# Order of the small matrix products in a one-core RWKV-7 and band-attention step: 64-row and 32-row products issued in turn on different parts of the TensorE array

## The chip, the cores and the metric

The kernel runs on one core of one Trainium2 chip. The metric is the device time of one execution in microseconds (us); lower is better. Engines are named as the profile names them: PE is TensorE's products, PEld its weight loads, DVE is VectorE, ACT is ScalarE, POOL is GpSimd, SP is the engine whose queue issues nearly all DMAs. Times inside an execution are microseconds from the start of its span.

## What is computed

One inference step of a two-layer encoder for two request groups: a prompt of 1024 tokens, and 8 sequences of 16 new tokens that continue older states. The width is 1024, with 16 heads of 64 features in both layers.

```python
# layer 0: recurrence with a 64x64 state a head
sa = einsum('bhij,bhj->bhi', s, a_t)
s  = s * w_t[:, :, None, :] + sa[..., None] * b_t[:, :, None, :] + v_t[..., None] * k_t[:, :, None, :]
y  = einsum('bhij,bhj->bhi', s, r_t)
out = (group_norm(y) + bonus) * g @ w_o
# layer 1: attention over the own chunk of 64 tokens and the 8 chunks before it
s = einsum('bqhd,bkhd->bhqk', q_b, k_b) * scale + bias
p = softmax(where(allowed, s, NEG_INF))
o = einsum('bhqk,bkhd->bqhd', p, v_b)
# after each mix
x = x + gt_f * (silu(h @ w_gate) * (h @ w_up)) @ w_down
```

All arithmetic is fp32; the large products split each operand into a high part and a rest in a one-pass format (`F32R`), and the small ones are plain fp32 products, which the trace shows as two weight loads and two products each.

## The kernel before, in words

**Stages.** From 0 to about 1420 us: layer 0's projections in three blocks of 384 tokens (the third holds the last 256 of the prompt and the 128 of the samples), with the recurrence of earlier blocks beside them. Then the output projection, the gated feed-forward (1545 to 2400 us), keys, values and first queries (to 2640 us), the attention (2640 to 3210 us), and the second feed-forward.

**The recurrence** works on windows of 128 tokens, two chunks `c` of 64 tokens each, and on half of the heads at a time: four feature tiles `f`, each with two heads `e` (rows 0 to 63 and rows 64 to 127). There are 9 windows `w` (the last holds the samples) and so 18 units. `inverses` prepares a triangular inverse a chunk. `win_prep` (line 714) loads a unit's operands and makes the pairwise products `G` (lines 738 to 747: products with 64 rows and 128 columns of the array, four of one head half into a bank, then two DVE copies under a mask out of it), then transposes `BK` (lines 750 to 757). The banks of tag `G` are two. `win_state` (line 838) carries the state over a chunk with products `X`, `U`, `D` in banks of tag `st`, which take the two heads of a feature tile in turn on the left and the right half of the array's columns. `win_y` (line 902) sums a unit's output in one bank `Y`: for each `c`, `f`, `e` first a product over 128 rows (`YL`, `UV`) and at once the product of the state over 64 rows (`XL`, `S`; for the samples four products of 16 columns with `ssv`) onto the same columns. `win_post` normalises `Y`. `windows` weaves a unit's run with the end of the unit before, and prepares two units ahead.

**The attention** goes through eight pairs of heads (`pair`, line 1548). A tile is 128 queries `qt` of one head `e` against up to five blocks of keys. `advance` (line 1580) is a pipeline of tiles: at each step the new tile's scores (banks `S`) and exponentials, the output products of the tile three steps older, two steps of a later pair's queries (banks `acc`), then the transposes into `PT` (one buffer) and their copy to `pts` (two buffers, line 1633) of the tile one step older. The tile's output (line 1637) is up to five products in a row into the 64 columns of its own head. The order of a pair's 16 tiles is written out at line 1564: the second head one block of queries behind the first. After the first head's last tile the next pair's second head of keys and queries is loaded and split (`kprep`, `qprep`, lines 1426 and 1437). Two groups of four sample sequences a pair (`sample_group`, line 1667) enter the same pipeline; their output takes, for each sequence `b`, four products over 128 rows (`vc`, `pts`) into that sequence's quarter of 32 columns and one over 16 rows (`vn`, `pts`) onto it. The cache tiles `kc` and `vc` have one buffer each.

**What sets the order.** The kernel is written in a tile language that makes all waits and buffer assignments. Its planner replays the program in a simulated time before it is compiled, and lets each engine's queue take what is ready, the earlier in the code first. So the order in the code is a priority, and the order on an engine can differ from it. Each engine then runs its own queue in order.

Of the kernel before, what the change touches and what calls it, by code (L numbers as in the profile page):

```python
# [21 lines left out]
# ---------------------------------------------------------------- constants  # L22
# [54 lines left out]
def prep(i):  # L77
    i = {k: np.asarray(v) for k, v in i.items()}
    d = {}
# [7 lines left out]
    # groups of 16 tokens, each behind the token before it  # L87
# [17 lines left out]
    st = i["state_wkv"][0].transpose(3, 1, 0, 2)  # j, h, b, i  # L105
# [35 lines left out]
class Trunk:  # L141
# [11 lines left out]
    # ------------------------------------------------------------ set-up  # L153
# [34 lines left out]
    # ------------------------------------------------------------ adaLN  # L188
    def step(self, n=1):
        """n loads of the adaLN products that run beside other work"""  # L190
        for _ in range(n):
            next(self.ada, None)

    def ada_steps(self, units, tag="aux", bufs=1):
        """modulations, 512 features a unit: [128, 4, prompt and 8 sequences]; a quarter of a bank's rows sums two k tiles"""
# [22 lines left out]
    def gain(self, name, sc):  # L218
        """-(1 + scale) * norm gain / 2 in the scale's place, [128, 8, 9]"""
        A = self.mod[:, sc:sc + 8, :]  # L220
        g = self.P(name).rearrange("p (f o) -> p f o", o=1).broadcast_to([128, 8, 9])
        self.nc.vector.scalar_tensor_tensor(A, A, 1.0, g, ALU.add, ALU.mult)
        self.nc.vector.tensor_scalar(A, A, -0.5, None, ALU.mult)
        return A

    # ------------------------------------------------------------ weights
# [5 lines left out]
    def half(self, src):  # L232
        """half a weight unit as high part and rest"""
# [10 lines left out]
    def wunit(self, wp, src, n=1024, rows=128):  # L244
        """a weight unit as high part and rest"""
# [17 lines left out]
    def gemm(self, out, W, hi, lo, m=128):  # L263
        """out[m, 384] = W^T x over 8 k tiles; W = (hi, lo) units [128, 8*m]"""
# [5 lines left out]
    # ------------------------------------------------------------ norm  # L270
# [3 lines left out]
    def sq_add(self, st, x, gp=False):  # L274
        """adds the squares of a tile of 128 features"""
# [10 lines left out]
    def sq_done(self, st):  # L286
        """-2 / rms"""
# [12 lines left out]
    def rsqrt2(self, r, ss, u, n, e):  # L300
        """r = -2 (ss / n + eps)^-1/2, n = 4^i (one Newton step after exp(-ln(v)/2)); u is scratch"""
# [7 lines left out]
    def rsqrt(self, r, v, u):  # L309
        """r = v^-1/2 (one Newton step after exp(-ln(v)/2)); u is scratch"""  # L310
# [8 lines left out]
    def normed(self, x, r, A, sh0, f):  # L319
        """x * r * A + shift of a feature tile, in place; per feature for the prompt, per feature and sequence for the samples"""  # L320
# [17 lines left out]
    # ------------------------------------------------------------ RWKV projections  # L338
    def proj_open(self, ctx):
# [5 lines left out]
        self.hb = pp.tile([128, 8, 408], F32, name="hb")  # 24 groups of 16 tokens, each behind the token before it  # L345

    def hgroups(self, t):
        """views of the tokens and of the tokens before them"""
# [3 lines left out]
    def lora_weights(self):  # L352
        """low-rank input weights scaled by 1 - mix and by mix, to scratch"""
# [64 lines left out]
    def mixed(self, m, b):  # L418
        """h + (h_prev - h) * mix, split"""
# [42 lines left out]
    def proj(self, b):  # L462
        """the projections of a block; the next one's inputs are prepared before a projection's products"""
# [25 lines left out]
    def proj_r(self, b, hi, lo):  # L489
        """decayed receptances, and the bonus r k summed over a head"""  # L490
# [19 lines left out]
    def proj_lora(self, b, hi, lo):  # L510
        """decay, in-context rate and gate; a low-rank product's high and low parts share a pass"""
# [67 lines left out]
    def proj_v(self, b, hi, lo):  # L579
        """values token-major, and the bonus times the values"""  # L580
# [23 lines left out]
    def spans(self, b):  # L604
        """(columns, columns with one more before each chunk, chunk, index of the first chunk)"""
# [4 lines left out]
    def proj_k(self, b, hi, lo):  # L610
        """keys, removal keys and values-to-remove, with the decay before (a~) and the decay's inverse (b^, k^)"""
# [42 lines left out]
    # ------------------------------------------------------------ chunked RWKV-7  # L654
    def win_open(self, ctx):
        nc = self.nc
        self.wp = ctx.enter_context(self.tc.tile_pool(name="win", bufs=1, reuse_waits="tile"))
        # inverses of the 16x16 diagonal blocks (a block a partition), and their way into 64x64 block matrices
# [5 lines left out]
        for i in range(2):  # L664
            zf = self.Z[i].rearrange("c g i -> (c g i)").rearrange("(u p x) -> u p x", u=2, p=128)
            for u in range(2):
                nc.sync.dma_start(zf[u], z)
        self.eends = [self.wp.tile([128, 8, 12], F32, name=f"eend{b}") for b in range(NB)]
# [12 lines left out]
    def win_first(self, w, hf, ld):  # L681
        """the products of b^ with a~"""
# [22 lines left out]
    def inverses(self, b):  # L705
        """(I - A)^-1 of a block's chunks"""
        self.TT = getattr(self, "TT", {})
        for w in range(3 * b, 3 * b + 3):
            ld = self.dp.tile([64, 2, 2, 8, 64], F32, tag="ld", name=self.nm("ld"), bufs=2)  # s, half, parity, (c, pair), t
# [4 lines left out]
    def win_prep(self, w, hf):  # L714
        """everything else of 2 chunks x 8 heads that does not depend on the state"""
# [18 lines left out]
        # pairwise products  # L734
# [3 lines left out]
        for c in range(2):  # L738
            for e in range(2):
                G = self.bank("G", 2)  # L740
                h = slice(64 * e, 64 * e + 64)
                for f in range(4):
                    mm(nc, G[:, f * 128:(f + 1) * 128], bkv[h, f, c], xl[h, e:3:2 - e, 2 * f + c, :], True, True)
                gv = G.rearrange("p (f x t) -> p f x t", f=4, x=2)
# [3 lines left out]
        # token-major b^, k^  # L748
        bkt = ring("BKT", [128, 2, 2, 256], nr)
        for e in range(2):  # L750
            pt = self.bank("G", 2)
            h = slice(64 * e, 64 * e + 64)
            for c in range(2):
                for f in range(4):
                    o0 = (c * 4 + f) * 64
# [1043 lines left out]
```

## Time and profile before

| what | value |
|---|---|
| median of 3 runs (lowest, highest) | 4096.49 us (4077.86, 4105.21) |
| span of the profiled execution | 4087.3 us |
| mean granted TensorE clock | 0.924 of full speed |
| DVE busy / ACT busy / POOL busy | 2275.8 / 1579.8 / 625.1 us |
| DMA | 554.22 MB, mean 136 GB/s |

The profiled execution has no time of its own beside its span; the span lies within the three runs, 9 us below their median.

How to read the rows: in a group of instructions, `Y<-YL,UV 128*64 128x64 f32 x576 | 100.1, 259` means products into tile Y from tiles YL and UV, with 128 rows and 64 columns of the array in use, 64 columns of output streamed over 128 partitions, 576 of them; they cover 100.1 us of the span together, and one lasts 259 ns from its start to its end. Products overlap in the array, so what one adds to PE's time is the covered time by the count, or the distance of starts in the timeline. A plain fp32 product appears twice. In a timeline row the first number is the start, the second the length of the merged piece. In a row of windows the columns are the stretch, its length, the busy time of each engine with its instructions, the granted clock, and the share of the DMA engines.

### The profile page before, as it was taken

The page shows a single profiled execution, that of the slowest core. Times are in us where ns is not written, and L with a number is a line of the kernel's source. Part 1 is how long each engine was busy: PE and PEld are TensorE (multiplying, and loading weights), DVE is VectorE, ACT ScalarE, POOL GpSimd, SP SyncE. Part 2 cuts the span into 40 slices and gives each one's busy share as a digit, 9 for nine tenths or more (in the row PEclk, how much of TensorE's full clock was granted, in tenths as well). Part 3 has the DMA queues.
Part 4 walks back from the last instruction along what each step waited for, and adds up shares of the span by engine and source line. Part 5 has one row for each costly group of instructions (what it writes and reads, how often), then busy time and mean ns, then how long its engine had stood idle before and what let it go on. Part 6 is the DMA issues. An engine that isn't in the chain of part 4 may idle for free.

```text
span 4087.3 us, 71391 instructions
## 1 busy us (share of the span) xinstructions
PE 3796.6 (93%) x28196; PEld 3275.0 (80%) x28196; DVE 2275.8 (56%) x4259; ACT 1579.8 (39%) x2986; POOL 625.1 (15%) x569
## 2 busy tenths in 40 slices
PE   5898998999899979999999999899999979999999
PEld 3676777777666769999977878777777879999998
DVE  3666466565423485455355762455556665454567
ACT  4644455554212253333421254455554443333410
POOL 0000000000000055445200110100000155454000
PEclk8796898789668879999999999999999989999999
DMA  5783575467645432222555313244355422222522
GB/s 198 226 245 86 174 232 166 136 176 231 172 116 160 135 119 79 76 75 74 189 196 184 124 59 103 88 147 137 122 153 170 147 88 78 76 74 76 178 83 76
DMA packets 430208, 554.22 MB, mean 136 GB/s; under 512 B 128528, under 2 KB 297872, under 8 KB 425392
## 3 DMA queue, kind: packets, MB, share of 16 engines
q1 hardware_dynamic: 375728, 530.77, 41.4%
q10 hardware_dynamic: 54144, 18.89, 2.0%
q8 instruction: 222, 3.64, 0.4%
q14 instruction: 114, 0.93, 0.1%
HBM read 415.39 MB, written 134.12 MB: 134 GB/s over the span
## 4 chain that ended last, share of the span: by engine, by line
PE 78%; DMA 8%; DVE 7%; ACT 3%; issue 2%; POOL 1%; SPq 1%; ACTq 0%; DVEq 0%; POOLq 0%
PE S L138 30%; PE PT L138 16%; PE acc L138 15%; PE st L138 4%; PE Y L138 4%; PE O L138 3%; PE G L138 2%; PE aux L138 2%; DMA raw<-in_wada 1%; DVE h L255 1%; PE PT L1632 1%; DMA sp_v<-vv 1%; DMA h<-out_kT 1%; DVE wlo L255 1%; DVE t L799 0%
## 5 line engine op out<-in xcount | busy, mean ns | idle before, releaser
L138 PE MATMUL S<-h,w 128*128 128x320 f32 (+1 forms) x4944 | 693.0, 299 | 14.6 <-DVE h L255 4.5
L138 PEld LDWEIGHTS S<-h,w 128*128 128x128 f32 x4944 | 672.6, 191 | 22.4 <-DVE h L255 8.2
L138 PE MATMUL acc<-mx,whi 128*128 128x384 f32 (+1 forms) x1824 | 534.6, 372 | 51.2 <-ACT whi L254 22.5
L138 PE MATMUL S<-h,wh 128*128 128x320 f32 (+1 forms) x2844 | 532.8, 339 | 13.7 <-DVE h L1013 6.1
L138 PEld LDWEIGHTS S<-h,wh 128*128 128x128 f32 x2844 | 458.2, 190 | 82.5 <-DVE h L1258 13.4
L138 PEld LDWEIGHTS acc<-mx,whi 128*128 128x128 f32 (+1 forms) x1824 | 347.2, 199 | 88.8 <-ACT whi L254 24.7
L254 ACT ACTIVATE w<-rq 128x512 fp32r<-128x512 f32 x308 | 192.0, 629 | 501.7 <-PE S L138 196.7
L255 DVE TENSOR_TENSOR w<-rq,w 128x512 fp32r<-128x512 f32 x308 | 271.0, 884 | 201.8 <-ACT w L254 201.2
L138 PE MATMUL PT<-h,w 128*128 128x320 f32 (+1 forms) x2448 | 351.2, 298 | 19.3 <-ACT w L254 7.6
L138 PEld LDWEIGHTS PT<-h,w 128*128 128x128 f32 x2448 | 333.7, 190 | 23.7 <-ACT w L254 8.0
L138 PE MATMUL acc<-mx,wlo 128*128 128x384 f32 (+1 forms) x912 | 330.4, 363 | 5.9 <-DVE wlo L255 5.9
L138 PE MATMUL PT<-h,wh 128*128 128x320 f32 (+1 forms) x1428 | 285.0, 343 | 4.1 <-DVE h L1368 1.4
L1191 POOL TENSOR_TENSOR t<-t,t 128x576 f32<-128x576 f32 (+1 forms) x132 | 215.3, 1631 | 412.9 <-ACT t L1198 295.4
L138 PEld LDWEIGHTS PT<-h,wh 128*128 128x128 f32 x1428 | 232.6, 189 | 39.6 <-DVE h L1258 6.9
L138 PEld LDWEIGHTS acc<-mx,wlo 128*128 128x128 f32 (+1 forms) x912 | 180.8, 198 | 19.3 <-DVE wlo L255 8.9
L255 DVE TENSOR_TENSOR wlo<-raw,whi 128x1024 fp32r<-128x1024 f32 (+1 forms) x123 | 146.2, 1190 | 75.0 <-ACT whi L254 73.4
L254 ACT ACTIVATE whi<-raw 128x1024 fp32r<-128x1024 f32 (+1 forms) x123 | 125.6, 1023 | 154.1 <-PE acc L138 116.4
L255 DVE TENSOR_TENSOR h<-h,h 128x1024 fp32r<-128x1024 f32 (+4 forms) x112 | 123.2, 1113 | 78.4 <-ACT h L254 61.5
L254 ACT ACTIVATE h<-h 128x1024 fp32r<-128x1024 f32 (+4 forms) x112 | 103.0, 934 | 163.1 <-DMA h<-sd 112.4
L254 ACT ACTIVATE wh<-rq 128x512 fp32r<-128x512 f32 x124 | 74.6, 626 | 231.0 <-PE S L138 144.0
L1258 DVE TENSOR_TENSOR h<-h,S 128x640 f32<-128x640 f32 (+1 forms) x150 | 111.9, 750 | 91.3 <-PE S L138 91.0
L1191 DVE TENSOR_TENSOR t<-S,t 128x576 f32<-128x576 f32 (+1 forms) x116 | 86.4, 744 | 124.6 <-PE S L138 124.5
(393 smaller groups left out, 6120.1 us busy)
## 6 DMA issues: line engine op xcount, KB each, us to landing
h<-in_wada SPq DMA_DIRECT2D x64, 512.0 KB, 6.6
raw<-in_wada SPq DMA_DIRECT2D x48, 512.0 KB, 4.5
rq<-in_wg SPq DMA_DIRECT2D x88, 256.0 KB, 2.6
rq<-in_wu SPq DMA_DIRECT2D x88, 256.0 KB, 2.7
rq<-in_wd SPq DMA_DIRECT2D x88, 256.0 KB, 3.0
kc<-in_ck SPq DMA_DIRECT2D x16, 1024.0 KB, 5.2
vc<-in_cv SPq DMA_DIRECT2D x16, 1024.0 KB, 5.5
sd<-t SPq DMA_DIRECT2D x88, 160.0 KB, 1.9
```

The costliest lines, as they stand in the source:

```text
L138: return nc.tensor.matmul(out, lhsT, rhs, start=start, stop=stop)
L254: self.nc.scalar.activation(hi, x, AF.Copy)
L255: self.nc.vector.tensor_tensor(lo, x, hi, ALU.subtract)
L1191: eng.tensor_tensor(out, x, y, ALU.add)
L1258: nc.vector.tensor_tensor(y, y, d, ALU.add)
L1632: nc.tensor.transpose(pt[:, j * 128:(j + 1) * 128], P[:, j * 128:(j + 1) * 128], self.C("ident"))
```

## The change

Five places, beside comments that go:

- `win_prep`: the pairwise products of a chunk now fill both `G` banks, the two heads of a feature tile in turn (rows 0 to 63, rows 64 to 127), and both banks are emptied after that. The transposes of `BK` do the same.
- `win_y`: a product of zeros (new tile `zr`, 128x128, one-pass format, made once in `win_open`) opens the whole bank `Y`. Then come all products over 128 rows, then all products of the state over 64 rows; all of them add.
- `pair`: the two heads' tiles of the same queries are now neighbours in the order.
- `tile`: the first head's tile leaves its transposed weights in `self.even` and returns; the second head's tile makes the output products of both, in turn on the two halves of the columns. `pts` keeps its two buffers.
- `sample_group`: the products with `vc` go through the four quarters in turn, and the four products with `vn` follow at the end.

The diff without the lines that only lose comments:

```diff
@@ win_open
+        self.zr = self.wp.tile([128, 128], F32R, name="zr")
+        nc.scalar.activation(self.zr, z[:, 0:128], AF.Copy)
@@ win_prep
         for c in range(2):
+            Gs = [self.bank("G", 2) for _ in range(2)]
+            for f in range(4):
+                for e in range(2):
+                    h = slice(64 * e, 64 * e + 64)
+                    mm(nc, Gs[e][:, f * 128:(f + 1) * 128], bkv[h, f, c], xl[h, e:3:2 - e, 2 * f + c, :], True, True)
             for e in range(2):
-                G = self.bank("G", 2)
-                h = slice(64 * e, 64 * e + 64)
-                for f in range(4):
-                    mm(nc, G[:, f * 128:(f + 1) * 128], bkv[h, f, c], xl[h, e:3:2 - e, 2 * f + c, :], True, True)
-                gv = G.rearrange("p (f x t) -> p f x t", f=4, x=2)
+                gv = Gs[e].rearrange("p (f x t) -> p f x t", f=4, x=2)
                 nc.vector.tensor_tensor(yl[:, c, e], gv[:, :, 1, :], mr, ALU.mult)
                 h2 = slice(64 * (1 - e), 64 * (1 - e) + 64)
                 nc.vector.tensor_tensor(xl[h2, e, c::2], gv[h2, :, 0, :], ma[h2], ALU.mult)
         bkt = ring("BKT", [128, 2, 2, 256], nr)
+        pt = [self.bank("G", 2) for _ in range(2)]
+        for c in range(2):
+            for f in range(4):
+                for e in range(2):
+                    o0 = (c * 4 + f) * 64
+                    h = slice(64 * e, 64 * e + 64)
+                    nc.tensor.transpose(pt[e][:, o0:o0 + 64], bkv[h, f, c], self.C("ident")[h, h])
         for e in range(2):
-            pt = self.bank("G", 2)
-            h = slice(64 * e, 64 * e + 64)
-            for c in range(2):
-                for f in range(4):
-                    o0 = (c * 4 + f) * 64
-                    nc.tensor.transpose(pt[:, o0:o0 + 64], bkv[h, f, c], self.C("ident")[h, h])
-            nc.scalar.activation(bkt[:, :, e], pt.rearrange("p (c f d) -> p c (f d)", c=2, f=4), AF.Copy)
+            nc.scalar.activation(bkt[:, :, e], pt[e].rearrange("p (c f d) -> p c (f d)", c=2, f=4), AF.Copy)
@@ win_y
         Y = self.bank("Y", 1)
-        for c in range(2):
-            for f in range(4):
-                for e in range(2):
-                    c0 = f * 128 + c * 64
-                    mm(nc, Y[hs[e], c0:c0 + 64], R.uv[:, c, e, f, :], R.yl[:, c, e, f, :], True, False)
-                    r = R.xl[hs[e], 2, 2 * f + c, :]
-                    if w == 8:
-                        for g in range(4):
-                            mm(nc, Y[hs[e], c0 + 16 * g:c0 + 16 * g + 16], R.sv[c][hs[e], f, g, :], r[:, 16 * g:16 * g + 16],
-                               False, g == 3)
-                    else:
-                        mm(nc, Y[hs[e], c0:c0 + 64], R.S[c][hs[e], f, :], r, False, True)
+        order = [(c, f, e) for c in range(2) for f in range(4) for e in range(2)]
+        mm(nc, Y, self.zr, self.zr.rearrange("p (o t) -> p o t", o=1).broadcast_to([128, 4, 128]), True, False)
+        for c, f, e in order:
+            c0 = f * 128 + c * 64
+            mm(nc, Y[hs[e], c0:c0 + 64], R.uv[:, c, e, f, :], R.yl[:, c, e, f, :], False, False)
+        for c, f, e in order:
+            c0 = f * 128 + c * 64
+            r = R.xl[hs[e], 2, 2 * f + c, :]
+            if w == 8:
+                for g in range(4):
+                    mm(nc, Y[hs[e], c0 + 16 * g:c0 + 16 * g + 16], R.sv[c][hs[e], f, g, :], r[:, 16 * g:16 * g + 16],
+                       False, (c, f, g) == (1, 3, 3))
+            else:
+                mm(nc, Y[hs[e], c0:c0 + 64], R.S[c][hs[e], f, :], r, False, (c, f) == (1, 3))
@@ pair
-        order = sorted((qt + e, e, qt) for e in range(2) for qt in range(8))
+        order = [(e, qt) for qt in range(8) for e in range(2)]
         groups = self.samples(n)
-        for i, (_, e, qt) in enumerate(order):
+        for i, (e, qt) in enumerate(order):
@@ tile
         yield
+        if not e:
+            self.even = pts
+            return
         O = self.O[:, qt // 2 % 2 * 256:qt // 2 % 2 * 256 + 256]
         oc = slice(qt % 2 * 128, qt % 2 * 128 + 128)
         for j in range(nk):
-            mm(nc, O[h, oc], vf[:, k0 + j, h], pts[:, j * 128:(j + 1) * 128], j == 0, j == nk - 1)
-        if qt % 2 and e:
+            for u, p in enumerate((self.even, pts)):
+                hu = slice(64 * u, 64 * u + 64)
+                mm(nc, O[hu, oc], vf[:, k0 + j, hu], p[:, j * 128:(j + 1) * 128], j == 0, j == nk - 1)
+        if qt % 2:
             self.heads_out(n, (qt - 1) * 128, O)
@@ sample_group
         O = self.wide_bank("PT", 1)
-        for b in range(4):
-            bs = slice(b * 32, b * 32 + 32)
-            for j in range(4):
+        quarters = [(b, slice(b * 32, b * 32 + 32)) for b in range(4)]
+        for j in range(4):
+            for b, bs in quarters:
                 mm(nc, O[bs, 0:128], pts[:, j * 128 + b * 32:j * 128 + b * 32 + 32], vc[:, b, j], j == 0, False)
+        for b, bs in quarters:
             mm(nc, O[bs, 0:128], pts[0:16, 512 + b * 32:512 + b * 32 + 32], vn[:, b], False, True)
```

## The prediction

> **What bounds the kernel now.** I read the page's busy times first, then the granted clock, then the busy times in the stretches that the change touches.
>
> ```profile
> span 4087.3 us, 71391 instructions
> ...
> PE 3796.6 (93%) x28196; PEld 3275.0 (80%) x28196; DVE 2275.8 (56%) x4259; ACT 1579.8 (39%) x2986; POOL 625.1 (15%) x569
> ...
> PEclk8796898789668879999999999999999989999999
> ```
>
> ```profile
> 340.00:1000.00 660.00, 623.97 (x5894) 500.44 (x5893) 393.35 (x853) 326.16 (x624) 10.74 (x49) 0.88 0.60 175
> 1000.00:1180.00 180.00, 160.47 (x1807) 120.93 (x1810) 72.64 (x188) 48.76 (x101) 0.00 (x0) 0.74 0.59 164
> 1180.00:1420.00 240.00, 230.92 (x1592) 171.37 (x1588) 96.52 (x195) 57.71 (x99) 0.00 (x0) 0.81 0.44 133
> 2640.00:3210.00 570.00, 529.93 (x3900) 434.27 (x3901) 332.80 (x985) 284.29 (x648) 2.40 (x16) 0.98 0.48 147
> ```
>
> PE is covered for 93% of the span, and in both stages that the change touches (recurrence beside the projections, 340 to 1420; attention, 2640 to 3210) no other engine comes near it: DVE has 52% (1000 to 1420: 40%) and 58%. So time taken out of PE's queue there is mostly time taken out of the span. The small products are dear for what they compute. These are their groups, shapes kept apart:
>
> ```profile
> L138 PE MATMUL O<-pts,vf 128*64 128x128 f32 x960 | 134.9, 283 | 0.1
> ...
> L138 PE MATMUL Y<-YL,UV 128*64 128x64 f32 x576 | 100.1, 259 | 1.3 <-DVE UV L869 1.3
> L138 PE MATMUL G<-XL,BK 64*128 64x128 f32 x576 | 90.0, 345 | 2.0 <-DMA BK<-sp_k 1.6 <-DVE XL L747 0.4
> L138 PE MATMUL Y<-XL,S 64*64 64x64 f32 x512 | 87.4, 253 | 0.0
> ...
> L138 PE MATMUL PT<-vc,pts 128*32 128x128 f32 x512 | 67.9, 276 | 4.0 <-ACT pts L1633 3.7
> ...
> L138 PE MATMUL Y<-XL,ssv 64*64 64x16 f32 x256 | 30.8, 252 | 0.0
> L138 PE MATMUL st<-UV,BKT 128*64 128x64 f32 x512 | 30.5, 249 | 3.5 <-ACT UV L870 2.4 <-DVE UV L869 1.0
> ...
> L756 PE MATMUL G<-cst,BK 64*128 64x64 f32 x288 | 25.9, 255 | 2.0 <-issue 1.3 <-ACT BKT L757 0.7
> ```
>
> The same shape, 128 rows by 64 columns by 64, costs 174 ns a record in Y (100.1 / 576) and 60 ns in st (30.5 / 512). In st the two halves of the columns take turns and no other shape stands between. That ratio is what the change is about.
>
> **Part 1, Y (L902).** The timeline shows both orders side by side, at two granted clocks:
>
> ```profile
> 420.32 1.11 PE L138 MATMUL st<-UV,BKT 128*64 128x64 f32 x14
> 421.22 0.42 PE L138 MATMUL Y<-YL,UV 128*64 128x64 f32 x2
> ...
> 422.78 0.47 PE L138 MATMUL Y<-YL,UV 128*64 128x64 f32 x2
> 423.19 0.47 PE L138 MATMUL Y<-XL,S 64*64 64x64 f32 x2
> ```
>
> ```profile
> 437.20 0.68 PE L138 MATMUL st<-UV,BKT 128*64 128x64 f32 x14
> 437.72 0.28 PE L138 MATMUL Y<-YL,UV 128*64 128x64 f32 x2
> ...
> 438.18 0.33 PE L138 MATMUL Y<-YL,UV 128*64 128x64 f32 x2
> 438.44 0.33 PE L138 MATMUL Y<-XL,S 64*64 64x64 f32 x2
> ```
>
> ```profile
> 420.30:424.50 4.20, 4.20 (x32) 3.25 (x32) 0.85 (x2) 1.61 (x4) 0.00 (x0) 0.50 0.60 201
> 437.20:440.00 2.80, 2.80 (x35) 2.19 (x33) 0.85 (x2) 0.49 (x2) 0.00 (x0) 1.00 0.61 193
> ```
>
> Each change of shape starts 0.26 us after the last one at full clock, 0.41 at half, with two records in it. Fourteen records in turn take at most 437.72 - 437.20 = 0.52 us, 37 ns each, and at half clock 0.90 us, 64 ns. So a change of shape costs about 0.26 - 0.07 = 0.19 us (half clock 0.28). A unit has 16 products of each kind: 8.2 us now at full clock, 12.9 at half; the rows say (512 x 0.174 + 87.4) / 16 = 11.0, so 40% of it runs at full clock. After: 64 records at that mix (53 ns) are 3.4 us, three changes 0.7, and the new product of zeros, priced by the one-pass products of 512 columns:
>
> ```profile
> L138 PE MATMUL S<-h,wh 128*128 128x512 f32 x804 | 207.4, 401 | 6.2 <-DVE h L1013 6.1
> ```
>
> 207.4 / 804 = 0.26 us, 0.35 at the mix. That is 4.5 us; a unit gives back 6.5, sixteen units **104**. The two sample units have (64 x 0.174 + 30.8) / 2 = 21.0 us now; 32 records at 53 ns, 128 short ones at about 60 (they take 120 now with one change for every eight) and 1.1 for the rest are 10.5, so **21** more. Bounds for Y: 90 and 145, by 64 and 37 ns a record.
>
> **Part 2, G (L742) and the transposes (L756).** No row shows two row halves in turn over all columns. Nearest is O and st, where two halves overlap fully: by them 90.0 falls to 45, 25.9 to 13. From the other side, if the halves don't overlap, nothing is won, and something can be lost: both banks are now filled before either is emptied, so the next chunk's products wait for four DVE copies of 0.42 us instead of two:
>
> ```profile
> L745 DVE TENSOR_TENSOR YL<-G,cst x72: 397/424/426, 345.8 to 1238.5; 128x256 f32<-128x256 f32 x72
> ```
>
> That is up to 0.85 us twice a unit, 31 us for 18 units, where no projection products (acc) stand ready to fill it. I take 40 and 12, near the rows where halves overlap, since the planner has acc work until 1180. Bounds -31 and +58.
>
> **Part 3, O (L1641).** 134.9 / 960 = 140 ns a record with one half always idle; in turn 70: **67**.
>
> ```profile
> L138 PEld LDWEIGHTS O<-pts,vf 128*64 128x64 f32 x960 | 103.7, 139 | 23.4 <-issue 21.1 <-DVE P L1627 0.7 <-DVE h L255 0.3
> ```
>
> And 64 of 128 changes of shape go, at 21.1 / 128 = 0.16 us each: **11**. Bounds 0 and 85; I take 78, by st.
>
> **Part 4, sample outputs (L1710).** Quarters in turn have a precedent too:
>
> ```profile
> 2668.12 1.06 PE L138 MATMUL PT<-vc,pts 128*32 128x128 f32 x8
> 2669.11 0.13 PEld L138 LDWEIGHTS PT<-vn,pts 16*32 16x32 f32 x2 [0.20 <-issue]
> ...
> 2669.45 1.06 PE L138 MATMUL PT<-vc,pts 128*32 128x128 f32 x8
> ```
>
> ```profile
> 2684.02 1.08 PE L138 MATMUL S<-kc,qbd 128*32 128x512 f32 x8
> 2684.90 0.25 PE L138 MATMUL S<-ksm,qbd 128*32 128x16 f32 x8
> ```
>
> The scores take the quarters in turn: eight records of 512 columns in 0.88 us, 110 ns each, while the outputs, eight records of only 128 columns in one quarter, take 2669.11 - 2668.12 = 0.99. A group now is 4 x (2669.45 - 2668.12) = 5.3 us. After: 32 records at about 33 ns, 8 at 33, two changes of 0.2: 1.7. Saved 3.6 x 16 = **57**; if only two quarters overlap (60 ns), 43.
>
> The Trainium skill, page TensorE: Matmul & The Clock Gate, section "Part 3: Packing small matmuls — row/col tiling", says that a weight load overlaps running products only when its row group differs. By that rule column halves and quarters over 128 rows would gain nothing but the fewer changes of shape. The kc rows speak against it: same rows, different quarters, 110 ns for 512 columns.
>
> **Sum of PE time taken out:** 104 + 21 + 40 + 12 = 177 in the recurrence, 78 + 57 = 135 in the attention, 312 in all.
>
> **What of it is kept.** Recurrence, 1000 to 1420 us, rows of tile Y and of tile G:
>
> ```profile
> 1000.00:1420.00 420.00, 82.02 (x608) 65.17 (x608) 4.18 (x7) 0.78 0.50 147
> ```
>
> ```profile
> 1000.00:1420.00 420.00, 45.77 (x352) 39.81 (x352) 20.64 (x50) 7.92 (x14) 0.78 0.50 147
> ```
>
> Here few projection products are left to put into the recurrence's own waits. Of Y's 218 us 82.0 lie here, of G's 116 up to 45.8, so some 65 of the 177. There PE already stands idle 29 of 420 us. I let half of the 65 be lost (33) and a tenth of the rest (11): 133 kept. Attention: two costs.
>
> First, the new order of tiles moves the load of the next pair's second head from behind tile 13 to behind tile 14, and brings its first use from the third tile to the second.
>
> ```profile
> 2772.82 2.15 SPq L1433 DMA_DIRECT2D h<-out_kT  x2
> ...
> 2785.83 1.22 DVE L255 TENSOR_TENSOR h<-h,h 64x1024 fp32r<-64x1024 f32 x1
> ...
> 2790.77 0.44 PE L138 MATMUL S<-h,h 128*128 128x128 f32 x2
> ```
>
> From issue to operands ready: 2787.05 - 2772.82 = 14.2 us, used at 2790.77, 18 us after. Three steps after the change (570 us / (8 x 18 steps) = 4.0 us now, about 3.2 then) are 9.6, so it is 4.6 us late at seven borders: 32 if nothing else can run, 15 as I take it, because queries and the first head's tiles are ready. What queues behind the late scores on PE is that head's tile only, as the planner sees the load.
>
> Second, `pts` keeps two buffers, and both now wait for the pair's output; the next copy to `pts` and the transposes behind it in `PT` come later.
>
> ```profile
> PE PT L1632 <- ACT pts L1633: 15.9, 15, 4.5
> ```
>
> PE waits 15.9 us for that copy now; I add 10 (bounds 0, and 0.7 for each of 64 pairs of tiles, 45). The vc load, queued on SP behind the old products, goes out earlier. Kept: 135 - 25 = 110.
>
> Together 133 + 110 = 243: the span falls from 4087.3 to 3844. The median of the runs is 9 us above that span, which gives 3853; I say **3850**.
>
> **The rivals.** The first two differ by what covers PE's waits, the third and fourth by what the chip and the planner make of the order, the last is on the other side.
> (a) All of it is kept, since PE is the only full engine: 4096 - 312 = 3784. For it: DVE and ACT under 60%. Against: the recurrence's chain.
> (b) The cover is gone: the chains of recurrence and softmax set the time once PE is shorter; 40% kept, 125, so 3971. For it: in either stage DVE or ACT empties each small bank before PE's next step in that chain; against: PE idles only 36 of 660 us (340 to 1000) and 40 of 570 now.
> (c) The planner undoes the order: it takes what is ready, and the first head's products are ready before the second's (as at 437.72 Y products stand between st products). Then O saves nothing and Y half of its 125: 312 - 78 - 62 = 172, at 0.78 kept 134: 3962.
> (d) Column parts don't overlap: O keeps 11, the quarters 20 (six changes of 0.2 us in 16 groups), Y loses 23 (576 records by 40 ns that no longer hide): 312 - 67 - 37 - 23 = 185, kept 144: 3952. The skill's rule above would give that; the trace speaks against it.
> (e) Slower, by the clock:
>
> ```profile
> 780.00:1000.00 220.00, 212.88 (x1738) 169.44 (x1735) 120.41 (x257) 105.45 (x206) 6.15 (x30) 0.93 0.68 199
> ```
>
> Regrouped products leave PE's queue emptier, and the clock is lowest where PE is idle most (0.74 in 1000 to 1180). From 340 to 1420 PE has 1015 us of work at a mean of 0.84; 177 less is 838. If the clock fell under 0.84 x 838 / (838 + 312) = 0.61 there, the whole gain would be lost; at 0.58, 838 x 0.84 / 0.58 - 838 = 376 more, 4096 - 312 + 376 = 4160. For it: the dips exist; against: where PE is fullest it is not low (780 to 1000: 97%, 0.93), and the change removes just the work that uses the array least.
>
> **How the numbers follow.** Forecast 0.52 (its own range 3790 to 3910), (a) 0.14, (b) 0.14, (c) 0.07, (d) 0.04, (e) 0.05; the last 0.04 is a loss of most of the gain to late keys and G's banks together, within 1%. A measurement of this kernel tells about 1% from no change. Faster by over 1%: 0.52 + 0.14 + 0.14 + 0.07 + 0.04 = 0.91; same 0.04; slower 0.05. The range leaves out (e), the 0.04, and a tail of (a) and (b): 3750 to 3985.
>
> **What would show it.** Right: Y's records fall from 174 to about 55 ns and one wide zero product stands before each unit; O from 140 to about 70 ns in groups of up to 20; vc from 133 to about 33; G from 156 to about 85; attention near 460 us. Wrong: O in groups of ten again (c); records shorter but idle time before PE up by over 100 us (b); a mean clock under 0.85 of the whole (e); new waits of PE for h of L255 at pair borders beyond 15 us.

## The result, and the profile after

The changed kernel takes 3959.1 us (median of four runs, 3951.49 to 3962.81), the kernel before 4089.52 (four runs, 4077.86 to 4105.21). The ratio is 0.9668, with a 95% interval of 0.9636 to 0.97: about 136 us faster at 4096.49. The forecast was 3850 us, that is 243 us, in a range of 3750 to 3985. The direction held; a little over half of the gain came.

The page of the kernel after, its busy times and the granted clock in 40 slices:

```profile
span 3955.1 us, 71500 instructions
...
PE 3611.2 (91%) x28214; PEld 3130.9 (79%) x28214; DVE 2269.6 (57%) x4259; ACT 1581.1 (40%) x2987; POOL 634.3 (16%) x569
...
PEclk8787798799679779999999999989999999999999
```

PE gave up 185.4 us (3796.6 to 3611.2). The span fell by 132.2, since PE's idle time rose from 290.7 to 343.9 us. DVE, ACT and the clock (0.918 in the mean, 0.924 before) hardly moved.

The groups of PE in the kernel after (busy us, mean ns of one, idle before them), for the rows shown of before:

```profile
L138 PE MATMUL O<-pts,vf 128*64 128x128 f32 x960 | 99.9, 297 | 1.5 <-ACT pts L1640 1.5
...
L138 PE MATMUL G<-XL,BK 64*128 64x128 f32 x576 | 77.5, 332 | 5.7 <-DMA XL<-sp_r 2.0 <-issue 1.9 <-PE aux L138 0.8
...
L138 PE MATMUL Y<-YL,UV 128*64 128x64 f32 x576 | 38.5, 239 | 0.0
...
L759 PE MATMUL G<-cst,BK 64*128 64x64 f32 x288 | 26.6, 259 | 1.4 <-ACT BKT L761 0.7 <-DVE XL L750 0.6
...
L138 PE MATMUL Y<-XL,S 64*64 64x64 f32 x512 | 18.5, 222 | 0.0
...
L138 PE MATMUL PT<-vc,pts 128*32 128x128 f32 x512 | 17.3, 276 | 7.7 <-ACT pts L1640 7.7
...
L138 PE MATMUL Y<-zr 128*128 128x512 f32 x18 | 13.3, 740 | 2.4 <-ACT zr L669 2.4
L138 PE MATMUL Y<-XL,ssv 64*64 64x16 f32 x256 | 12.5, 221 | 0.0
...
L138 PE MATMUL PT<-vn,pts 16*32 16x128 f32 x128 | 6.7, 280 | 0.0
```

The mean length of one product stays as it was. What shrinks is the time that all of a group cover together, that is, how far they overlap. Against the terms of the prediction (the `vn` group took 25.7 us before):

| term | PE time forecast | PE time measured |
|---|---|---|
| Y, zero product included | -125 | 218.3 to 82.8: -135 |
| G, pairwise products | -40 | 90.0 to 77.5: -12 |
| G, transposes | -12 | 25.9 to 26.6: +1 |
| O, grouping and changes of shape | -78 | 134.9 to 99.9: -35 |
| sample quarters (`vc`, `vn`) | -57 | 93.6 to 24.0: -70 |
| sum | -312 | -252 |

Y and the quarters came in a little above the forecast, G and O far below it. Of the 252, PE as a whole shows 185: neighbouring groups overlap at their ends, so that the groups' sum counts some time twice (the product of zeros is such a case, see below), and other groups stood in more time at a lowered clock (the projections' `acc<-mx` groups 11 us more).

The windows of the kernel after (length, then busy time of PE, PEld, DVE, ACT and POOL, clock, DMA share, GB/s), cut where the same work lies:

```profile
340.00:1000.00 660.00, 595.62 (x6095) 482.97 (x6093) 399.23 (x867) 340.16 (x647) 14.99 (x49) 0.86 0.63 184
1000.00:1107.00 107.00, 78.74 (x1153) 56.88 (x1151) 49.84 (x138) 23.74 (x54) 0.00 (x0) 0.67 0.61 175
1107.00:1346.00 239.00, 230.52 (x2047) 171.40 (x2041) 111.40 (x235) 69.02 (x121) 0.00 (x0) 0.84 0.51 156
2566.00:3078.00 512.00, 445.11 (x3918) 362.85 (x3919) 337.01 (x988) 285.04 (x652) 2.48 (x16) 0.95 0.54 165
```

The recurrence now ends near 1346 us instead of 1420, the attention takes 512 us instead of 570. New idle time of PE: beside the projections (340 to 1000) 64 us where 36 were; from 1000 to the recurrence's end 37 where 29 were; in the attention 67 where 40 were.

PE's waits in the attention of the kernel after (us in total, times, the longest):

```profile
PE PT L1639 <- ACT pts L1640: 22.6, 28, 3.4
PE PT L1639 <- DVE so L1733: 14.5, 10, 3.5
PE acc L138 <- ACT wh L254: 9.8, 2, 9.2
PE PT L138 <- ACT pts L1640: 7.7, 7, 1.6
PE PT L1714 <- ACT pts L1640: 2.8, 6, 0.6
...
PE O L138 <- ACT pts L1640: 1.5, 2, 0.9
...
PE S L138 <- DVE h L255: 0.4, 1, 0.4
```

The waits for the `pts` copy (L1640, L1633 before) went from 15.9 + 3.7 = 19.6 us to 22.6 + 7.7 + 2.8 + 1.5 = 34.6 us. The scores' wait for a late split of the keys, of which the prediction was afraid, is 0.4 us, once.

### The profile page after: what moved, and what is told of

Its sections match the earlier page's. It is cut to its first block, busy times and chain, and to the rows that moved or that the text cites. A ratio compares the mean times of both kernels' runs of the same rounds, so it can differ in the third digit from the quotient of the medians.

```text
span 3955.1 us, 71500 instructions
## 1 busy us (share of the span) xinstructions
PE 3611.2 (91%) x28214; PEld 3130.9 (79%) x28214; DVE 2269.6 (57%) x4259; ACT 1581.1 (40%) x2987; POOL 634.3 (16%) x569
## 4 chain that ended last, share of the span: by engine, by line
PE 69%; DMA 12%; DVE 8%; ACT 5%; issue 3%; POOL 1%; SPq 1%; ACTq 0%; DVEq 0%; POOLq 0%
PE S L138 30%; PE PT L138 15%; PE acc L138 14%; PE st L138 4%; PE O L138 2%; DMA raw<-in_wada 1%; PE PT L1639 1%; PE G L138 1%; DVE h L255 1%; PE Y L138 1%; PE aux L138 1%; DMA TT<-Z 1%; DVE wlo L255 1%; DMA sp_r<-rr 1%; DMA Z<-T 1%
## 5 line engine op out<-in xcount | busy, mean ns | idle before, releaser
L255 DVE TENSOR_TENSOR w<-rq,w 128x512 fp32r<-128x512 f32 x308 | 270.1, 881 | 203.0 <-ACT w L254 202.4
L255 DVE TENSOR_TENSOR wlo<-raw,whi 128x1024 fp32r<-128x1024 f32 (+1 forms) x123 | 145.8, 1186 | 110.0 <-ACT whi L254 108.3
L255 DVE TENSOR_TENSOR h<-h,h 128x1024 fp32r<-128x1024 f32 (+4 forms) x112 | 122.9, 1112 | 88.6 <-ACT h L254 74.3
```

Source lines behind the costliest of these rows:

```text
L255: self.nc.vector.tensor_tensor(lo, x, hi, ALU.subtract)
```

## The experiments

**The four parts, one at a time.** Each takes one part of the diff into the kernel before and leaves the rest of it.

```diff
 e1: win_y and win_open (zr) of after
 e2: win_prep of after
 e3: pair and tile of after
 e4: sample_group of after
```

> Only the recurrence's outputs are regrouped (zero product, then all 128-row, then all 64-row products); the rest is as before. Theory A (PE time taken out counts by about half in the recurrence, since waits at the borders of the blocks don't move): tile Y falls from 218 to about 83 us of PE time, the span by 55 to 80 us, 4010 to 4035 us. Rival B (regrouping the pairwise products G costs what Y gains, so Y alone gains more): 90 to 125 us, 3965 to 4000. Rival C (the recurrence's chain sets its time, and nearly all of the gain came from the attention): under 30 us, above 4060.

> Only the pairwise products and the transposes of the recurrence are regrouped. Theory A (the planner issues one half's four products as soon as its bank is free, so more than half of them still run one half at a time): 10 to 15 us less PE time in G, span within 15 us of before, 4075 to 4105. Rival B (both banks filled before either is emptied costs time): 15 to 40 us slower. Forecast on record had 40 + 12 us less PE time: 30 to 50 us faster.

> Only the attention's tiles are reordered and the two heads' outputs are made in turn. Theory A (each pair of tiles starts with a lone product of the first head that the planner takes early, and PE waits more for the copies to pts): O from 135 to about 100 us of PE time, span 15 to 35 us shorter, 4055 to 4075. Rival D (late keys and the two pts buffers take all of it): within 10 us of before. Forecast on record: 78 less 25, 50 us shorter.

> Only the sample groups' outputs go through the quarters in turn. Theory A: 70 us less PE time in 16 bursts (5.3 us to about 1.4 each), of which half to four fifths are kept: 35 to 55 us shorter, 4035 to 4055. Rival E (the bursts ran while something else had to be waited for anyway): under 20 us.

| part alone | ratio to before, interval | us |
|---|---|---|
| Y | 0.9752, 0.9719 to 0.9786 | -102 |
| G | 1.0028, 1.001 to 1.0045 | +11 |
| O with its order | 0.9969, 0.9951 to 0.9987 | -13 |
| quarters | 0.9887, 0.9857 to 0.9917 | -46 |
| sum of the four | | -150 |
| all together | 0.9668, 0.9636 to 0.97 | -136 |

The parts add up within the noise, so most of what is missing lies within parts, not between them. Spreading what the prediction kept in each stage over its terms in proportion, Y was to bring 94 us, G 39, O 64 and the quarters 46. Y and the quarters brought about that. G and O fell short by 50 and 51 us.

Not all of a part's gain is its PE time, as the granted clock differs too. With Y alone its mean is 0.933 to 0.936 in the four runs, against a median of 0.922 in the kernel before. The rise lies in the recurrence behind the projections: 0.86 from 990 to 1340 us, where PE is covered for 310.9 us, against 0.78 from 1000 to 1420 before. At 0.78 the same work would take some 32 us longer (an estimate: 310.9 x (0.86 / 0.78 - 1)). In the kernel after, the clock there is 0.78 again (1000 to 1346). With the quarters alone the attention runs at 0.96, against 0.98 before. Why the clock moves so is open, and no run separates it from the order of the products.

**Why G brings nothing.** The timeline of PE in the kernel after shows both orders, the first at a clock of 1.00, the last three rows while half the clock was granted:

```profile
365.65 1.17 PE L138 MATMUL G<-XL,BK 64*128 64x128 f32 x16
366.75 0.55 PE L138 MATMUL acc<-mx,whi 128*32 128x384 f32 x2
...
389.64 1.13 PE L138 MATMUL G<-XL,BK 64*128 64x128 f32 x8 [0.44 <-DMA BK<-sp_k]
390.69 0.44 PE L138 MATMUL acc<-ag,whi 128*128 128x384 f32 x1
...
396.04 2.07 PE L138 MATMUL G<-XL,BK 64*128 64x128 f32 x8
398.05 0.69 PE L138 MATMUL acc<-ag,whi 128*128 128x384 f32 x1
...
398.67 1.64 PE L138 MATMUL G<-XL,BK 64*128 64x128 f32 x6
```

At 365.65 the two halves took turns: 16 records in 1.10 us, 69 ns each. At 389.64 one half alone fills its bank: 8 records in 1.05 us, 131 ns each (251 ns at 396.04, at half clock). So row halves do overlap, but most of the products still don't go in turn. Counted in the traces, 238 of G's 576 records in the kernel after start within 20 ns of another one, 118 in the kernel before. The likely reason is the planner: the first of the two `G` banks comes free before the second, its four products are ready, and they are taken.

Nor was the kernel before without overlap. Its queue often holds the fillings of the two halves one right behind the other:

```profile
373.91 1.71 PE L138 MATMUL G<-XL,BK 64*128 64x128 f32 x16
375.55 0.37 PE L138 MATMUL acc<-mx,whi 128*32 128x384 f32 x1
```

Here 16 records take 375.55 - 373.91 = 1.64 us, 102 ns each at full clock: the second half starts while the first still runs. So there was less to win than the 131 ns of one half alone suggest.

To test this, both banks became one tile that is waited for and released as a whole, in the kernel after:

```diff
-            Gs = [self.bank("G", 2) for _ in range(2)]
+            Gw = self.wide_bank("G", 1)
+            Gs = [Gw[:, 512 * e:512 * e + 512] for e in range(2)]
...
-        pt = [self.bank("G", 2) for _ in range(2)]
+        Gw = self.wide_bank("G", 1)
+        pt = [Gw[:, 512 * e:512 * e + 512] for e in range(2)]
```

> The changed kernel with both G banks as one tile of one buffer, so that both come free together: no product of one half can start ahead of the other's, and all 288 pairwise products and the 288 transposes stand in turn. Theory A (the planner's runs of four undo G's regrouping, and in turn two row halves do overlap): G's PE time falls from 77 to about 50 us and the transposes' from 27 to 16. The span: 10 to 25 us shorter if PE's time counts; longer by up to 20 if the wait for four copies out of G between two fillings is not covered.

The groups of this kernel, and PE's waits in its recurrence:

```profile
L138 PE MATMUL G<-XL,BK 64*128 64x128 f32 x576 | 61.5, 343 | 10.0 <-DMA BK<-sp_k 4.8 <-DVE XL L751 3.6 <-DMA XL<-sp_r 1.1
...
L761 PE MATMUL G<-cst,BK 64*128 64x64 f32 x288 | 16.4, 261 | 4.2 <-DVE XL L751 4.2
```

```profile
PE acc L138 <- ACT mx L254: 32.3, 8, 14.6
PE st L138 <- DVE t L805: 21.7, 19, 8.7
...
PE G L138 <- DMA pa<-sp_b: 18.4, 5, 8.2
```

Now 412 of the 576 records start within 20 ns of another one, and G costs 77.9 us where 104.1 stood, and yet the ratio is 0.9738 (0.9709 to 0.9768), 26 us above the kernel after (3985.43). PE's waits for `mx`, `t` and `pa` are 72.4 us together; the same rows of the kernel after, over its recurrence, are 17.6, 13.8 and 9.6, 41.0 together. So the turn comes when the banks come free together, and what it wins in PE is paid for, and more, in waits. This run also joins the bank of `inverses` with them (its group `G<-pa` takes 30.3 us, 23.7 in the kernel after), so its price is an upper one for the change itself.

The other check leaves G as it was, with all other parts in:

```diff
 after, with win_prep of before
```

> The changed kernel with win_prep as before. Theory A (regrouped G costs about 11 us, as alone): 8 to 14 us shorter than the changed kernel, 3945 to 3951. If G's cost came only from its own disturbance of the old schedule: within 4 us.

Measured 0.9644 (0.9622 to 0.9666), 3948.53 us: some 10 us better than the kernel after. The two intervals overlap, so this run alone doesn't settle the sign. In the kernel before, e2's +11 does, as its interval lies above 1. The group of G in e8:

```profile
L138 PE MATMUL G<-XL,BK 64*128 64x128 f32 x576 | 79.2, 319 | 8.4 <-DMA XL<-sp_r 5.6 <-issue 1.8 <-DVE XL L749 0.9
```

Ungrouped it takes 79.2 us here, grouped 77.5 after: with Y regrouped, the order that came out saves next to nothing. With Y alone, G's old code takes 80.8 us instead of 90.0, so with Y in, G's own regrouping gives only some 2 to 3 of the 12 us in the table of terms. In e2's profile the group falls to 77.2 us, but PE as a whole is busy as long as before (3797.1 against 3796.6 us).

**O: the order, the lone product, the buffers.** First the order of tiles alone, in the kernel before; then the same with the loads of the next pair's second head written earlier, behind the tiles 11 and 12 of a pair (before they stood behind tile 13):

```diff
-        order = sorted((qt + e, e, qt) for e in range(2) for qt in range(8))
+        order = [(e, qt) for qt in range(8) for e in range(2)]
```

```diff
+            if i == 11 and n < 7:
+                self.raws["k", n + 1, 1] = self.kload(n + 1, 1)
+            if i == 12 and n < 7:
+                self.raws["q", n + 1, 1] = self.qload(n + 1, 1)
```

> The kernel before with only the new order of the attention's tiles (both heads of the same queries as neighbours); each tile still makes its own outputs. Theory F (the new order itself costs time, since the next pair's keys for the second head are loaded one step later and used one tile earlier): 10 to 35 us slower than before, 4107 to 4132, with more idle time of PE at the pair borders. Theory H (what O's grouping wins is lost to the two pts buffers and the lone first products, not to the order): within 8 us of before.

> As the run with only the new order of tiles (1.0055 of before), but the DMAs of the next pair's keys and queries for the second head are issued three and two tiles earlier, into scratch; only their split waits for the first head's last tile. Theory F1 (the order costs time because these loads, 6 us each, come late): at least half of its 22 us comes back, 4085 to 4104 us, ratio 0.997 to 1.003. If the order costs time by other means (which tiles stand beside which, the planner's whole sequence): 1.004 to 1.008, as without.

The order alone costs 1.0055 (1.0031 to 1.0078), 22 us. With the loads written early it costs 1.0047 (1.003 to 1.0064): the same. But the second run doesn't test what it was made for. Counted in the traces by the output records that PE has started, 14 of the 16 loads of a head's keys go out at the same point in both runs (after 70, 190, 310, 430 and 550 of the 960, for instance), whatever the code says. What speaks against the late keys is something else: the new order doesn't make them late. In the kernel before these five go out after 70, 190, 310, 429 and 550 records, and with the order alone PE shows no wait for their split (`h` of L255). So the prediction's 15 us for late keys name the wrong cause. PE's output products, first and last start, in the kernel with the order alone:

```profile
L138 PE MATMUL O<-pts,vf x960: 272/273/477, 2647.6 to 3217.4; 128*64 128x128 f32 x192
```

and before:

```profile
L138 PE MATMUL O<-pts,vf x960: 272/273/476, 2654.3 to 3204.2; 128*64 128x128 f32 x192
```

They span 569.8 us instead of 549.9, with the same products. In that stretch PE is covered 12 us longer and idle 8 us longer, at a granted clock of 0.97 instead of 0.99. The clock would account for most of the 12 (an estimate: 518.2 us of PE before, x (0.99 / 0.97 - 1) = 11), and PE's waits for the `pts` copy rise by 5. Why the order brings both about stays open. What follows is that grouping O brings 0.9969 / 1.0055, about 35 us, as much as its group's time shows, and that the order takes 22 of them away.

Second, why O's PE time fell by 35 and not by 78. PE's timeline in the kernel after:

```profile
2700.50 0.43 PE L138 MATMUL O<-pts,vf 128*64 128x128 f32 x2
2701.43 0.77 PE L1639 MATMUL PT<-cst,P 128*128 128x128 f32 x5 [0.50 <-ACT pts L1640]
2702.13 1.31 PE L138 MATMUL O<-pts,vf 128*64 128x128 f32 x18
2703.37 1.08 PE L138 MATMUL S<-kc,qbd 128*32 128x512 f32 x8
...
2718.36 1.08 PE L138 MATMUL PT<-vc,pts 128*32 128x128 f32 x32
2719.38 0.42 PE L138 MATMUL PT<-vn,pts 16*32 16x128 f32 x8
2719.72 0.43 PE L138 MATMUL O<-pts,vf 128*64 128x128 f32 x2
2720.09 0.74 PE L138 MATMUL S<-h,h 128*128 128x256 f32 x4
```

Eighteen records take 2703.37 - 2702.13 = 1.24 us, 69 ns each: the predicted 70. But the first product of each pair of tiles, two records, stands by itself ahead of that (2700.50, 2719.72). Its operand `self.even` is ready before the second head's, so the planner can let it go, and the others wait for the second head's transposes. It takes 2720.09 - 2719.72 = 0.37 us by itself where two records in turn take 0.14. So the outputs still stand in 128 separate groups, as many as before, where 64 were meant. If the second head's product is written first, nothing is ready early:

```diff
-            for u, p in enumerate((self.even, pts)):
+            for u, p in ((1, pts), (0, self.even)):
```

> The changed kernel, with the second head's product first in each step of the output loop. The planner can then start a pair's outputs only when the later transposes are there, and all of a pair's products stand together (32 groups of ten products instead of a lone one and nine). Theory H1 (the lone first products cost): 56 to 64 times 0.37 - 0.14 = 0.23 us, 13 to 15 us less PE time, 5 to 15 us shorter than the changed kernel: 3944 to 3954. If the lone product only filled a wait for the second copy to pts: within 4 us of it, with PE waiting more before O.

```profile
L138 PE MATMUL O<-pts,vf 128*64 128x128 f32 x960 | 75.6, 305 | 0.5 <-ACT pts L1640 0.5
```

The 64 groups are there now, and O falls from 99.9 to 75.6 us, by more than the 13 to 15 expected. The time does not fall: 0.9663 (0.9621 to 0.9706), not to be told from the kernel after. PE now waits longer for the copies to `pts`, 45.3 us instead of 34.6, as if the lone products had filled part of that wait. The output products:

```profile
L138 PE MATMUL O<-pts,vf x960: 272/273/477, 2569.4 to 3057.2; 128*64 128x128 f32 x192
```

They span 487.8 us; in the kernel after, by the same view, 2584.1 to 3076.9, 492.8.

Third, the buffers: three of `pts` instead of two, paid for in memory with two `ht` buffers less.

```diff
-        pts = self.att("pts", [128, 640], 2)
+        pts = self.att("pts", [128, 640], 3)
...
-... bufs={"xin": 2, "ht": 5}[tag])
+... bufs={"xin": 2, "ht": 3}[tag])
```

> The changed kernel with three buffers for pts instead of two (and three instead of five for ht, the scratch of the queries' norm, which makes the room). Theory H2 (the next copy to pts waits for a pair's outputs, and that gives O's gain back): PE's waits for pts fall from 33 us to under 15, the attention is 10 to 30 us shorter than in the changed kernel: 3930 to 3950. If the copies don't matter, or fewer ht buffers cost the same: within 5 us of 3959, or slower.

Measured 0.962 (0.9601 to 0.9639), 3941.18 us, some 18 us under the kernel after; the two intervals only just touch. Its output products:

```profile
L138 PE MATMUL O<-pts,vf x960: 272/273/476, 2581.3 to 3057.7; 128*64 128x128 f32 x192
```

They span 476.4 us instead of 492.8, and PE's waits for `pts` fall from 34.6 to 18.3 us, by as much. So the gain lies in the attention.

**Does PE's time still count?** The kernel after with Y's sums left out (only the product of zeros stays, so the recurrence's outputs are not computed):

```diff
-        mm(nc, Y, self.zr, ..., True, False)
-        for c, f, e in order:
...
+        mm(nc, Y, self.zr, ..., True, True)
```

> The changed kernel with the recurrence's outputs left out but for the product of zeros that opens the bank (so y of the recurrence is zero before its norm): another 70 us of PE time less (38.5 + 18.5 + 12.5). If PE's time is still what counts in the recurrence, at the rate of the run with Y alone (100 us kept of 135): 45 to 60 us shorter than the changed kernel, 3900 to 3915. If the borders of the blocks (loads, the solver on DVE) set the time by now: under 20 us, above 3940.

The ratio is 0.9508 (0.9488 to 0.9528), 64 us under the kernel after, for 38.5 + 18.5 + 12.5 = 69.5 us of products that no longer run; PE as a whole is busy 75.0 us less. So between 0.85 and 0.9 of that time is still time of the span, with the waits for these products' operands, which go too. A theory in which PE is no longer what counts, and the borders between blocks set the time, falls with this.

**The corrections together:** G as before, the second head's product first, three `pts` buffers.

> The changed kernel with three corrections that ran singly: win_prep as before (10 us), the second head's product first in the output loop (between 0 and 10 us), three pts buffers and three ht buffers (18 us). If they add: 3925 to 3935 us, ratio 0.957 to 0.961. If pts buffers and product order fill the same waits: 3930 to 3942, 0.960 to 0.963.

```profile
L138 PE MATMUL O<-pts,vf x960: 272/273/477, 2569.2 to 3041.1; 128*64 128x128 f32 x192
```

Measured 0.9549 (0.9523 to 0.9575), 3916.16 us: clearly better than the kernel after, by some 48 us, and than each correction alone. The three alone sum to about 30, but the second head's product first is known only within 17 us, so the 18 above the sum are not clear of noise. In the attention the corrections about add up: the outputs span 471.9 us, 20.9 less than in the kernel after, where the second head's product first gave 5.0 and the third buffer 16.4. The rest lies ahead of the attention, where the outputs start at 2569.2 instead of 2584.1. They start there with G ungrouped alone too, but also, at 2569.4, in the profiled execution with only the second head's product first, which changes nothing ahead of the attention. So these 15 us are no measure of a correction.

## Why the prediction was right in direction and half off in size

- **PE bounds it: held.** PE fell by 185 us and the span by 132; DVE and ACT did not take its place. Y left out shows PE's time still counting at 0.85 to 0.9.
- **Y: held in PE.** The forecast left 93 us of Y's 218 (16 units of 4.5, two of 10.5); 82.8 stand there. The products in turn were costed at 53 ns a record and the changes of shape apart; `Y<-YL,UV` takes 67 and `Y<-XL,S` 36, together 52 with the changes of shape in it. The product of zeros looks dearer than its 0.35 us (13.3 / 18 = 0.74), but it isn't, since it mostly runs beside the product ahead of it:

```profile
435.62 1.02 PE L138 MATMUL st<-y,cst 128*128 128x512 f32 x2
436.08 0.80 PE L138 MATMUL Y<-zr 128*128 128x512 f32 x1
436.81 0.68 PE L138 MATMUL st<-xs,TT 64*64 64x64 f32 x16
```

  Here `st` covers PE until 435.62 + 1.02 = 436.64 and `Y` until 436.08 + 0.80 = 436.88, 0.24 us more. Over all 18 the products of zeros add 6.5 us, 0.36 each. That Y's 102 us of time meet its 94 is in part luck: some 32 of them may be the clock's, as estimated above.
- **Quarters: held.** A group was costed at 1.7 us; it takes 2719.72 - 2718.36 = 1.36. Of the 70 us in PE 46 came out of the time, which is the amount that the prediction kept (46 of its 57). That the amounts agree is in part luck: more came out of PE than forecast, and a smaller share of it out of the time.
- **G: this step failed.** "I take 40 and 12, near the rows where halves overlap": the halves do overlap, at 69 ns a record, but 238 of 576 records go so, and the transposes gain nothing (25.9 to 26.6 us). The 90.0 us of before were not free of overlap either (102 ns a record where the two fillings stand side by side), so halving them asked for too much; and of the two precedents only `st` has its halves in turn, O before leaves one half idle. The second half of the step, "since the planner has acc work until 1180", failed too: the part costs 11 us by itself and 26 more when the turn is forced. Which wait costs the 11 is open. Its own bounds (-31 to +58) held this. Rival (c), the planner undoing the order, was put on O and Y. It came true on G, and on the first products of O.
- **O: the term was mis-sized.** 67 + 11 forecast, 35 measured in PE. The 70 ns a record are right; "64 of 128 changes of shape go" is wrong, as 64 new ones come with the lone first products. Of the 35 the order of the tiles took 22 away, against 15 for it: a size near the forecast with a cause that fell. For `pts` 10 were taken; the waits for its copy rose by 15.0 us. A third buffer is worth about 18, but the kernel before waited 19.6 us for that copy too, and no run gives it a third buffer, so how much of the 18 the change itself cost is open.
- **What is kept: wrong in its place.** The loss in the recurrence was set at 33 us from 1000 to 1420, where projection products run out. PE's idle time there rose by 8 us; beside the projections, where only a tenth was to be lost, it rose by 28. PE's longest waits from 160 to 1346 us in the kernel after:

```profile
PE aux L138 <- DMA raw<-in_wada: 19.8, 6, 14.3
PE acc L138 <- ACT mx L254: 17.6, 4, 15.6
PE st L138 <- DVE t L803: 13.8, 24, 3.4
```

The recurrence's own wait (`st` for `t`, 26.7 us before) became smaller. What grew is PE waiting for its supply: beside the projections one wait of 15.6 us for their mixed inputs (`mx`), and behind them, near 1047 us, one of 14.3 us for a load for the modulation (7.3 us before in all). In the attention idle time rose by 27 us, 15 of it for the `pts` copy.

- **The other rivals.** (a) falls: 185 us came out of PE as a whole and 136 out of the time. (b), 40% kept everywhere, lands near the measured time (3971) for the wrong reason: Y and the quarters bring what was forecast, and the shortfall is in G and O. (d) falls: column halves run at 69 ns a record, quarters at 2719.38 - 2718.36 = 1.02 us for 32 records, 32 ns each. So the Trainium skill's rule (page TensorE: Matmul & The Clock Gate, section "Part 3: Packing small matmuls — row/col tiling"), by which a load overlaps running products only in another row group, taken by itself does not agree with these traces: these products all use the same 128 rows. (e) falls as a loss of the gain: the mean clock is 0.918 against 0.924, and from 340 to 1346 the stretches lie near where they lay (0.86, 0.67 and 0.84; 0.88, 0.74 and 0.81 before). But the attention ran at 0.95 against 0.98, which is worth some 14 us of its 445 us of PE (an estimate: 445.1 x (0.98 / 0.95 - 1)).

## What to carry to other kernels

In this kernel, taking turns on parts of the array was worth a lot where the products share one bank and their operands are ready together (Y, the quarters), and nothing where each part waits for a bank of its own (G). Before costing such an order, ask for each product when its operand and its bank come free, and read the order in the trace, not in the code: what is ready alone can go alone (O's first products), and an earlier line for a load need not make it go out earlier. Look also at how far the products overlap already. A buffer that two tiles now hold at once belongs into the same edit. And take a group's busy time as what it covers, not as what it adds: the product of zeros covered 0.74 us and added 0.36.

## What the hardware showed that was not expected

- Two row halves over all 128 columns, each into a bank of its own, overlap when in turn: 69 ns a record of 128 columns against 131 for one half alone. Even where the code writes one half's four products ahead of the other's, as before, they can overlap in part, at 102 ns a record.
- Four column quarters in turn take 32 ns a record of 128 columns, half of what two halves take; one quarter by itself had taken 0.99 us for eight, 124 ns.
- The mean granted clock of this kernel differs between orders of the same products: 0.933 to 0.936 with Y alone, 0.918 to 0.921 with all parts, 0.913 to 0.919 with the quarters alone.
